# Layer-1 attention with keys and queries projected features-on-partitions, swap and second key form by transfers, rotation on GpSimd, and a new filling of the cells

## The chip, the cores and the metric

The kernel runs on one core of one Trainium2 chip. The metric is device time of one execution in microseconds, the median of several runs. Engines are named as in the profile: PE (TensorE matmul; PEld its weight loads), DVE (VectorE), ACT (ScalarE), POOL (GpSimd), SP (SyncE, which here issues nearly all transfers). Each engine runs its own instructions in order and waits on semaphores.

## The reference

A trunk of two layers over 512 latent tokens and 256 context tokens of width 1024. Layer 0 is a bidirectional mLSTM mixer, layer 1 a windowed attention; each is followed by a squared-ReLU MLP. The change concerns layer 1's mixer only:

```python
def project(u):
    q, k, v = jnp.split(u @ w_in, [1024, 1280], axis=-1)
    # 16 query heads, 4 key/value heads, 64 features each
cq, ck, cv = project(u_ctx)
lq, lk, lv = project(u_lat)
lq = _apply_rope(lq, cos, sin)      # latent tokens only
lk = _apply_rope(lk, cos, sin)

def _apply_rope(x, cos, sin):       # rotate pairs (j, j + 32)
    x1, x2 = x[..., :half], x[..., half:]
    return concatenate([x1 * cs - x2 * sn, x1 * sn + x2 * cs], axis=-1)
```

A block of 128 queries sees the key blocks beside it (distance up to 128) and all 256 context tokens, with a sink logit per head; the result goes through an output projection into the latent stream. Everything is float32; only the latent stream is returned.

## The kernel before

A float32 product is made of three matmuls of rounded halves (`mm3`): high by high, high by low, low by high. A weight unit of 128x1024 comes by a transfer on SP into one of three raw buffers; ACT casts it to whi (L1045) and DVE subtracts wlo (L1046), into one of four split slots. The matmuls of all such products have line L102, that of `mm3`.

Layer 1's mixer begins at the end of layer 0's MLP. `keys_begin` (L1630) projects keys and values of the context, `layer1_mix` (L1643) those of the latent tokens. Tokens lie on the partitions: the tokens' columns are the stationary operand and 256 weight columns move, so a block of 128 tokens gets its keys and values as 128x256 in PSUM (`proj_part`, L1847). In `kv_out` (L1870) and `q_out` (L1896) ACT copies V away; `rope` (L1856) makes two products on DVE and an addition on DVE or POOL (L1867); the result is split in halves (ksp, qsp: ACT cast L1883 and L1901, DVE subtraction L1884 and L1902), which are laid side by side for each head, 64 features of one half and 64 of the other. PE transposes them with identr, 128x128 at a time (48 transposes for the keys in L1890, 64 for the queries in L1907), and the copies ks (L1892) and qs (L1910) fetch them from PSUM. Keys exist in two forms, k0 (high half above, low half below for one, turned round for the other) and k1, so that two matmuls of 128 rows give the three products of halves.

Attention has 16 cells (g, j): head group g of four heads, query block j. `scores` (L1913) makes one head at a time: five or six matmuls into s (L1935 to L1942), the maximum on DVE (L1948), the exponential on ACT into e (L1955), and the division by the sum on POOL (L1966). `weigh` (L1970) transposes e on PE (L1982), copies it to ph on ACT (L1987) and makes the values' matmuls av (L1999, L2005); yb (L2007) and two DVE additions (L2010) put the result together.

The pattern `PAT = "SFTTFSFTFSTFTFSFFVVV"` sets the order within a cell: S a head of scores (five heads ahead of the cell), T transposes of one key block, V values, F a step of filling. The filling of PE's time is other projection work: in cells 0 to 3 the keys and values of head groups 2 and 3 (four steps), in every cell up to 13 the queries of a later cell (four steps of six matmuls of 256 columns, `q_steps`), and from cell 4 on two parts of the output projection of the group before (`out_part`, L1819), six in the last two cells. A scheduler orders each engine's instructions from the order in which the program makes them and from its own estimates of when their inputs are there; each engine then keeps that order.

Of the kernel before, what the change touches and what calls it, by code (L numbers as in the profile page):

```python
# [9 lines left out]
F32 = mybir.dt.float32  # L10
# [42 lines left out]
C_SN = C_CS + 4 * DH  # L53
C_END = C_SN + 4 * DH


class Trunk:
# [1036 lines left out]
    def ffn0(self, hooks, done, pre):  # L1094
# [219 lines left out]
        self.plan += [lambda pr=pr, i=i: self.unit(a["wskv"][pr, i]) for pr in range(2) for i in range(2)]  # L1314
# [315 lines left out]
    def keys_begin(self, u, hooks):  # L1630

        w = self.begun
        self.wkv = [w[:2], w[2:]]
        self.kvc = [self.mm.tile([P, 512], F32, name="pj", tag="mm") for _ in range(2)]
        at = {(1, 4, 0): 0, (1, 4, 2): 1}
        for pr in range(2):
            for j, t in zip((4, 5), self.kvc):
                for i in range(4):
                    self.proj_part(self.wkv[pr], j, self.rows_of(u), 256, i, t[:, 256 * pr:256 * pr + 256])
                    if (pr, j, i) in at:  # L1640
                        hooks[at[pr, j, i]]()

    def layer1_mix(self, u):  # L1643
        nc, tc, a = self.nc, self.tc, self.a
        self.ctx_ada.close()
        with tc.tile_pool(name="sw", bufs=1, reuse_waits="tile") as sw:
            cs = sw.tile([P, 4, DH], F32, name="cs")
            sn = sw.tile([P, 4, DH], F32, name="sn")
            nc.scalar.dma_start(out=cs.rearrange("p b d -> p (b d)"), in_=a["cst"][:, C_CS:C_CS + 4 * DH])
            nc.scalar.dma_start(out=sn.rearrange("p b d -> p (b d)"), in_=a["cst"][:, C_SN:C_SN + 4 * DH])  # L1650
            self.cs, self.sn = cs, sn
# [12 lines left out]
            ks = [sw.tile([P, 2, 2, T], F32R, name=f"ks{pr}") for pr in range(2)]  # L1664
# [5 lines left out]
            self.ptp, self.ptag = self.at, "at"  # L1670
            wkv, kvl = self.wkv, []
            for j, t in zip((4, 5), self.kvc):
                for pr in range(2):
                    kvl.append(self.kv_out(sw, pr, j, t[:, 256 * pr:256 * pr + 256], None))
            pss = [p_.tile([P, 512], F32, name="pj", tag=t_)[:, :256]
                   for p_, t_ in ((self.mm, "mm"), (self.mm, "mm"), (self.at, "at"), (self.at, "at"))]
# [4 lines left out]
            for f in kvl:  # L1681
                f()
            kvl = [self.kv_out(sw, 0, j, pss[j], nc.vector) for j in range(4)]
            late = []
            for j in range(2):
                ps = self.mm.tile([P, 512], F32, name="pj", tag="mm")[:, :256]
                for i in range(4):
                    self.proj_part(wq[0], j, rows, 256, i, ps)
                late.append(self.q_out(sw, 0, j, ps, nc.vector))
                for f in kvl[2 * j:2 * j + 2]:  # L1690
                    f()
            late.pop(0)()
            self.ctx_mm.close()
            with tc.tile_pool(name="sc", bufs=2, space=PSUM, reuse_waits="tile") as sc, \
                    tc.tile_pool(name="pt1", bufs=3, space=PSUM, reuse_waits="tile") as pt, \
                    tc.tile_pool(name="av", bufs=1, space=PSUM, reuse_waits="tile") as av:
                self.ptp, self.ptag = pt, "pt"
                ys = [None] * KVH
                todo = [(g, j) for g in range(KVH) for j in range(4)]
                qtodo = [(g, j) for g in range(KVH) for j in range(4)][2:]  # L1700
                parts = []

                def kv_steps(j):
                    ps = pt.tile([P, 512], F32, name="pj", tag="pt")[:, :256]
                    for i in range(4):
                        self.proj_part(wkv[1], j, rows, 256, i, ps)
                        yield
                    late.append(self.kv_out(sw, 1, j, ps, nc.gpsimd))

                def q_steps():  # L1710

                    if not qtodo:
                        return
# [452 lines left out]
```

## Time and profile before

| | |
|---|---|
| median of 3 runs | 1508.35 us (1508.11 to 1510.21) |
| profiled execution | 1506.92 us |
| its span | 1505.1 us |
| clock of PE, mean | 0.997 of full speed |
| layer-1 mixer in the trace, from its first projection to the last output parts | about 890 to 1172 us |
| first scores | 941.11 us |
| first values' matmuls of cells 0, 1, 13 and 14 | 958.88, 971.90, 1117.85 and 1128.82 us |

Time runs from the start of the span. A row of the profile gives line, engine, operation and the tiles written and read by the program's names; "out<-in". A window's row gives the busy time of each engine in it. A wait's row names what ended it. Since PE holds the sum of the time, one reads what PE does and where it stands.

### The profile page before, as it was taken

Reading aid. Unit: us, or ns where it says so; the run is one execution under the profiler, and the core shown is the slowest. Engines: PE = TensorE matmul, PEld = TensorE weight load, DVE = VectorE, ACT = ScalarE, POOL = GpSimd, SP = SyncE. Lnnn points to the kernel's source line nnn. Section 1 sums busy time; section 2 is a strip of 40 time slices with the busy share of each in tenths; the row PEclk is TensorE's granted clock in tenths of the full one; section 3 lists DMA queues with packets and bytes.
Section 4 is the critical chain, followed back from the end, with each engine's and each line's share of the span. In section 5 each row is a group of like instructions: output and inputs, shape, how many; then the busy total and the mean of one; then the engine's idle time right before and its main releaser. Section 6 shows DMA issues by size and latency. Waiting matters only on the chain.

```text
span 1505.1 us, 23719 instructions
## 1 busy us (share of the span) xinstructions
PE 1489.7 (99%) x9144; PEld 1332.4 (89%) x9145; DVE 1110.2 (74%) x2039; ACT 716.1 (48%) x1445; POOL 269.6 (18%) x275
## 2 busy tenths in 40 slices
PE   9999999999999999999999999999999999999998
PEld 5888898979899999999999999888877988888886
DVE  4986638497897877787777768676777874867697
ACT  4544243443764241432414345665666655545454
POOL 0112021311203223212232220323333000000000
PEclk9999999999999999999999999999999999999999
DMA  9233313245132334343443422010110533240321
GB/s 378 77 98 115 124 58 123 74 144 164 43 99 81 127 115 154 113 154 126 127 154 113 139 71 78 29 48 24 57 43 29 196 112 112 76 148 23 104 71 56
DMA packets 46632, 157.27 MB, mean 104 GB/s; under 512 B 5136, under 2 KB 7696, under 8 KB 46392
## 3 DMA queue, kind: packets, MB, share of 16 engines
q1 hardware_dynamic: 45344, 154.25, 31.1%
q8 instruction: 72, 1.18, 0.3%
q10 hardware_dynamic: 1175, 1.51, 0.3%
q14 instruction: 41, 0.33, 0.1%
HBM read 153.64 MB, written 2.10 MB: 103 GB/s over the span
## 4 chain that ended last, share of the span: by engine, by line
PE 93%; DVE 4%; ACT 2%; issue 1%; POOL 0%; POOLq 0%; DVEq 0%; ACTq 0%
PE mm L102 57%; PE p L102 10%; PE pj L102 5%; PE kept L102 3%; PE pt L1982 2%; PE pb L102 2%; PE pc L102 2%; PE av L1999 2%; PE acc L102 1%; PE at L1001 1%; PE s L1942 1%; PE at L958 1%; PE arow L102 1%; PE at L994 1%; PE s L1937 1%
## 5 line engine op out<-in xcount | busy, mean ns | idle before, releaser
L102 PE MATMUL mm<-h,whi 128*128 128x384 f32 x1024 | 262.5, 337 | 0.0
L1046 DVE TENSOR_TENSOR wlo<-raw,whi 128x1024 fp32r<-128x1024 f32 (+2 forms) x152 | 180.0, 1188 | 78.5 <-ACT whi L1045 76.7
L1045 ACT CAST whi<-raw 128x1024 fp32r<-128x1024 f32 (+2 forms) x152 | 150.9, 998 | 159.0 <-PE mm L102 105.9
L102 PE MATMUL mm<-uH,whi 128*128 128x512 f32 (+1 forms) x496 | 189.3, 386 | 0.0
L102 PE MATMUL mm<-uH,wlo 128*128 128x512 f32 (+1 forms) x496 | 186.7, 377 | 0.0
L102 PE MATMUL mm<-uL,whi 128*128 128x512 f32 (+1 forms) x496 | 186.0, 377 | 0.0
L102 PEld LDWEIGHTS mm<-h,whi 128*128 128x128 f32 x1024 | 185.4, 188 | 0.4 <-DVE h L1046 0.2
L269 DVE SCALAR_TENSOR_TENSOR adap<-raw,crow 128x1024 bf16<-128x1024 f32 x128 | 164.1, 1282 | 13.9 <-DMA raw<-ada 13.0
L102 PE MATMUL mm<-h,wlo 128*128 128x384 f32 x512 | 172.1, 336 | 0.0
L102 PE MATMUL p<-t,whi 128*128 128x384 f32 x448 | 114.2, 336 | 0.0
L1045 ACT CAST whi<-sum 128x512 fp32r<-128x512 f32 (+1 forms) x42 | 31.8, 760 | 162.2 <-PE mm L102 90.7
L102 PEld LDWEIGHTS mm<-uH,wlo 128*128 128x128 f32 x496 | 93.4, 188 | 17.4 <-issue 0.2
L102 PEld LDWEIGHTS mm<-uL,whi 128*128 128x128 f32 x496 | 93.5, 189 | 15.4 <-DVE uL L1091 0.3
L102 PEld LDWEIGHTS mm<-uH,whi 128*128 128x128 f32 x496 | 93.0, 189 | 15.2 <-issue 0.2
L102 PEld LDWEIGHTS mm<-h,wlo 128*128 128x128 f32 x512 | 96.1, 188 | 0.0
L1046 DVE TENSOR_TENSOR wlo<-wb,whi 128x1024 fp32r<-128x1024 f32 x49 | 59.1, 1219 | 36.0 <-ACT whi L1045 35.8
L1046 DVE TENSOR_TENSOR h<-r,h 128x384 fp32r<-128x384 f32 (+2 forms) x100 | 58.7, 589 | 31.2 <-ACT h L1045 30.8
L102 PEld LDWEIGHTS p<-t,whi 128*128 128x128 f32 x448 | 81.2, 188 | 0.0
L1045 ACT CAST whi<-wb 128x1024 fp32r<-128x1024 f32 x49 | 51.6, 1054 | 57.9 <-PE mm L102 48.2
L102 PE MATMUL mm<-uC,whi 128*128 128x256 f32 x416 | 78.2, 287 | 0.3 <-ACT whi L1045 0.3
L1966 POOL TENSOR_SCALAR e<-e,den 128x512 f32<-128x512 f32 (+1 forms) x64 | 51.4, 815 | 139.2 <-DVE den L1964 64.2
L102 PE MATMUL p<-t,wlo 128*128 128x384 f32 x224 | 75.3, 336 | 0.0
(405 smaller groups left out, 3626.2 us busy)
## 6 DMA issues: line engine op xcount, KB each, us to landing
raw<-ada SPq DMA_DIRECT2D x80, 512.0 KB, 3.5
raw<-w SPq DMA_DIRECT2D x64, 512.0 KB, 3.5
raw<-w2a SPq DMA_DIRECT2D x32, 512.0 KB, 3.5
wb<-w2b SPq DMA_DIRECT2D x28, 512.0 KB, 3.5
adaw<-ada SPq DMA_DIRECT2D x16, 512.0 KB, 11.2
raw<-wqk SPq DMA_DIRECT2D x8, 512.0 KB, 4.3
raw<-wv SPq DMA_DIRECT2D x8, 512.0 KB, 4.2
raw<-wo SPq DMA_DIRECT2D x8, 512.0 KB, 3.5
```

The source lines that it names most:

```text
L102: i = self.nc.tensor.matmul(**kw)
L269: self.tc.keep_in_program_order(nc.vector.scalar_tensor_tensor(out=pr, in0=w, scalar=0.5, in1=self.crow[:, v, :], op0=ALU.mult, op1=ALU.mu ...
L958: mm(out=kv[d][64 * h:64 * h + 64, n * VW:(n + 1) * VW], lhsT=kp[:, d, j, 64 * h:64 * h + 64], rhs=v[:, j, h, :], start=True, stop=True)
L994: mm(out=os[d][hh][:, ob], lhsT=qs[d][HP[hh], j * P:(j + 1) * P], rhs=C[HP[hh], n - 1, d, :], start=not started, stop=False)
L1001: mm(out=o[hh][:, i * VW:(i + 1) * VW], lhsT=pw[g, d, hh][:, i, :], rhs=v[:, 3 * g + i, hh, :], start=False, stop=i == 2)
L1045: keep(self.nc.scalar.copy(out=hi, in_=src))
L1046: keep((eng or self.nc.vector).tensor_tensor(out=lo, in0=src, in1=hi.bitcast(F32), op=ALU.subtract))
L1937: mm(out=lat, lhsT=ql, rhs=k0[:, lo * P:hi * P], start=True, stop=False)
L1942: mm(out=lat, lhsT=ql, rhs=k1[:, lo * P:hi * P], start=False, stop=True)
L1966: nc.gpsimd.tensor_scalar(out=out[ii][:, :W], in0=out[ii][:, :W], scalar1=den[:, ii:ii + 1], scalar2=1.0, op0=ALU.mult, op1=ALU.mult)
L1982: nc.tensor.transpose(out=pt[:, i * P:(i + 1) * P], in_=ps_[i][:, n * P:(n + 1) * P], identity=self.ident)
L1999: mm(out=o[i * DH:(i + 1) * DH, :], lhsT=v(n + i), rhs=pq[n + i], start=n == 0, stop=n == len(blks) - 2)
```

## The change

Keys and queries are projected turned: the weight columns (128 features, two heads) are stationary and 512 latent tokens move (256 for the context), so the result lies with features on the partitions (`turned`). V stays as it was (`values`). The weights are laid out for this on the host. No transposes of keys and queries are left; the tables of cosines and sines become 128x512.

Rotation needs each feature beside the one 32 partitions further. In `rope` with late=True (keys and all queries but those of group 0) ACT copies the product from PSUM to rt, four transfers of 32x512 on SP's queue write rx with the halves swapped, and POOL makes the two products and the addition at 128x512. With late=False (the queries of group 0) four ACT copies of 32x512 from PSUM make the swap, and DVE the three operations. `stack` splits two heads: for each an ACT cast of 64x512 and a DVE subtraction of 64x512 into the other 64 partitions. The second key form k1 is the first with its halves exchanged, by two transfers of 64 partitions per pair of heads. Buffers: e 12 to 10, qs now holds a head group (3 buffers), yb has its own two.

The filling is new. Blocks of queries of 128 features (eight steps of three matmuls of 512 columns) stand in cells 0, 1, 2, 3, 4 and 8; the values of blocks 2 and 3 are spread among the first five heads of scores; output parts go to cells 5 to 15 by a table. Matmul columns for K, Q and V are the same in sum: K and Q of the latent tokens are 48 and 192 matmuls of 128x512, V 96 of 128x256.

The order of ACT at the start of the attention, before: ksp and qsp are the split halves, pt the transposes, ks and qs the copies, whi a weight unit's cast, e the exponential of the first scores.

```order
L1045 CAST whi<-raw 128x1024
L1874 COPY vst_9547<-pj 128x128
L1045 CAST whi<-raw 128x1024
L1883 CAST ksp<-rp_9711 128x2x2x64
L1874 COPY vst_9545<-pj 128x128
L1892 COPY ks_9543<-pt 128x4x128
L1892 COPY ks_9542<-pt 128x4x128
L1892 COPY ks_9543<-pt 128x4x128
L1883 CAST ksp<-rp_9720 128x2x2x64
L1892 COPY ks_9542<-pt 128x4x128
L1883 CAST ksp<-rp_9729 128x2x2x64
L1892 COPY ks_9542<-pt 128x4x128
```

The same place after, up to the first exponentials: pk and pq are the products of keys and queries, pj those of the context, rt and rx the rotation's tiles, vst the values.

```order
L1879 CAST ks<-pj 64x256
L1045 CAST whi<-raw 128x1024
L1858 COPY rt<-pk 128x512 x2
L1879 CAST ks<-pj 64x256 x2
L1045 CAST whi<-raw 128x1024 x2
L1879 CAST ks<-rt 64x512 x2
L1864 COPY rx<-pq 32x512 x4
L1879 CAST ks<-rt 64x512 x2
L1864 COPY rx<-pq 32x512 x4
L1879 CAST qs<-rt 64x512 x2
L1673 COPY vst_9543<-pv 128x256
L1673 COPY vst_9544<-pv 128x256
```

The casts of the keys read rt, POOL's result, and stand ahead of the copies rx and the query casts; two whi casts stand ahead of them all.

SP's order at the same place, after (before, the weight units follow each other directly):

```order
L80 DMA raw<-wsq 128x1024 x3
L1887 DMA ks<-ks 64x2x256
L80 DMA raw<-wsq 128x1024
L1887 DMA ks<-ks 64x2x256 x3
L1862 DMA rx<-rt 32x512 x8
L80 DMA raw<-wsq 128x1024 x2
L1887 DMA ks<-ks 64x2x512 x4
L80 DMA raw<-wsq 128x1024 x2
```

The eight swap transfers stand behind the context's second key form, and the latent keys' behind the swaps.

POOL's order from the first rotation on, after. Before, the first thing it does here is the division of e (L1966), with a rotation's addition of 128x128 or 128x256 between groups of them.

```order
L1868 TENSOR_TENSOR rx<-rx,sn 128x512
L1869 TENSOR_TENSOR rt<-rt,cs 128x512
L1870 TENSOR_TENSOR rt<-rt,rx 128x512
L1868 TENSOR_TENSOR rx<-rx,sn 128x512
L1869 TENSOR_TENSOR rt<-rt,cs 128x512
L1870 TENSOR_TENSOR rt<-rt,rx 128x512
L1948 TENSOR_SCALAR e<-e,den 128x512 x4
L1948 TENSOR_SCALAR e<-e,den 128x640 x4
L1868 TENSOR_TENSOR rx<-rx,sn 128x512
L1869 TENSOR_TENSOR rt<-rt,cs 128x512
L1948 TENSOR_SCALAR e<-e,den 128x640 x2
L1870 TENSOR_TENSOR rt<-rt,rx 128x512
```

Six products of 128x512 stand ahead of the first division; later ones stand between the divisions.

The diff, cut to its core:

```diff
 def keys_begin(self, u, hooks):
-        w = self.begun
-        self.wkv = [w[:2], w[2:]]
+        self.wkv = w = self.begun
...
+        xs = self.xs(u)["C"]
+        for b in range(2):
+            self.turned(self.kvc[0][:, 256 * b:256 * b + 256], w[b], xs, 0, KT)
+        for j, at in ((4, slice(0, 256)), (5, slice(256, 512))):
+            for i in range(4):
+                self.values(self.kvc[1][:, at], j, self.rows_of(u), 2 * i, 2 * i + 2)
...
 def layer1_mix(self, u):
...
+            for m in range(2):
+                self.keys_out(m, self.kvc[0][:, m * NCX:(m + 1) * NCX], slice(NL, T))
...
             for kt in range(KT):
-                for j in range(4):
-                    self.proj_part(wkv[0], j, rows, 256, kt, pss[j], 1)
+                for b in range(2):
+                    self.turned(pk[b], self.wkv[b], xl, kt, kt + 1)
             wq = {0: [self.unit(a["wsq"][0, i]) for i in range(2)]}
...
+            rk = [self.rope(sw, pk[m], True) for m in range(2)]
+            for m in range(2):
+                ps = (self.at, self.mm)[m].tile([P, 512], F32, name="pq", tag=("at", "mm")[m])
+                self.turned(ps, wq[0][m], xl, 0, KT)
+                self.keys_out(m, rk[m](), slice(0, NL))
+                self.queries_out(sw, 0, m, self.rope(sw, ps, False))
...
+                qat = {0: (1, 0), 1: (1, 1), 2: (2, 0), 3: (2, 1), 4: (3, 0), 8: (3, 1)}
+                outs = {5: 3, 6: 3, 7: 2, 9: 3, 10: 2, 11: 2, 12: 2, 13: 3, 14: 6, 15: 6}
...
+                    ps = pt.tile([P, 512], F32, name="pq", tag="pt")
+                    for kt in range(KT):
+                        self.turned(ps, wq[g][b], xl, kt, kt + 1)
+                        if kt < KT - 1:
+                            yield
+                    late.append(lambda g=g, b=b, f=self.rope(sw, ps, True): self.queries_out(sw, g, b, f()))
...
                 def filler(n):
-                    fs, late[:] = late[:], []
-                    its = chain(kv_steps(n) if n < 4 else (), q_steps(), out_steps(2 if n < 14 else 6))
...
+                    its = chain(q_steps(*qat[n]) if n in qat else (), out_steps(outs.get(n, 0)))
+                    yield next(its, None)
+                    while late:
+                        late.pop(0)()
                     yield from its
...
-                for _ in range(4):
-                    next(sg)
...
+                fl = chain(v_steps(2, pt, "pt"), v_steps(3, pt, "pt"))
+                for _ in range(5):
+                    next(sg)
+                    next(fl, None)
+                    next(fl, None)
...
+    def turned(self, ps, w, xs, i0, i1):
+        for kt in range(i0, i1):
+            sl = slice(kt * P, (kt + 1) * P)
+            self.mm3(ps, w[0][:, sl], w[1][:, sl], *xs(kt), kt == 0, kt == KT - 1)
...
+    def rope(self, sw, ps, late):
...
+        x, y = [sw.tile([P, NL], F32, name=n, tag=n, bufs=2) for n in ("rt", "rx")]
+        if late:
+            nc.scalar.copy(out=x, in_=ps)
+        for i in range(4):
+            o, r = [slice(32 * k, 32 * k + 32) for k in (i ^ 1, i)]
+            if late:
+                nc.sync.dma_start(out=y[o], in_=x[r])
+            else:
+                nc.scalar.copy(out=y[o], in_=ps[r])
+        def rest():
+            op = (nc.gpsimd if late else nc.vector).tensor_tensor
+            op(out=y, in0=y, in1=self.sn, op=ALU.mult)
+            op(out=x, in0=x if late else ps, in1=self.cs, op=ALU.mult)
+            op(out=x, in0=x, in1=y, op=ALU.add)
+            return x
+        return rest if late else rest()
+
+    def stack(self, outs, x):
+        for e, out in enumerate(outs):
+            r, o = [slice(64 * i, 64 * i + 64) for i in (e, 1 - e)]
+            nc.scalar.copy(out=out[r], in_=x[r])
+            nc.vector.tensor_tensor(out=out[o], in0=x[r], in1=out[r].bitcast(F32), op=ALU.subtract)
+
+    def keys_out(self, m, x, cols):
+        k0, k1 = [self.swd["ks"][:, i, 2 * m:2 * m + 2, cols] for i in range(2)]
+        self.stack([k0[:, e] for e in range(2)], x)
+        for i in range(2):
+            self.nc.sync.dma_start(out=k1[64 - 64 * i:128 - 64 * i].bitcast(F32), in_=k0[64 * i:64 * i + 64].bitcast(F32))
```

The lines of the new functions that the traces name: L1858 the copy rt, L1862 the swap transfers, L1864 the copies rx, L1868 to L1870 the rotation, L1879 and L1880 the halves, L1887 the second key form, L1917 to L1924 the scores, L1930 the maximum, L1937 the exponential, L1948 the division, L1964 the transposes of e, L1969 ph, L1981 and L1987 the values, L1989 yb.

More of the change, by code (lines that the diff above doesn't have):

```diff
@@ L1313, in ffn0 @@
             self.plan += [unit_w2(c, i) for i in range(4)]
-        self.plan += [lambda pr=pr, i=i: self.unit(a["wskv"][pr, i]) for pr in range(2) for i in range(2)]
+        self.plan += [lambda i=i: self.unit(a["wskv"][i]) for i in range(4)]
         self.feed(True)
@@ L1663, in layer1_mix @@
                 msk.append(mk)
[L1664 removed]
+            ks = sw.tile([P, 2, KVH, T], F32R, name="ks")
             vst = [self.base.tile([P, 2, 2, DH], F32, name=f"vst{j}", tag=f"hC{j}") for j in range(NCH)]
@@ L1692, in layer1_mix, with v_steps @@
-            late.pop(0)()
+            rk = [self.rope(sw, pk[m], True) for m in range(2)]
[4 more added lines that the diff above has]
+                self.queries_out(sw, 0, m, self.rope(sw, ps, False))
+            def v_steps(j, pool, tag):
+                ps = pool.tile([P, 512], F32, name="pv", tag=tag)[:, :256]
+                for i in range(0, KT, 2):
+                    self.values(ps, j, rows, i, i + 2)
+                    if i < KT - 2:
+                        yield
+                put(j, ps)
+                yield
@@ L1896, in q_out @@
-    def q_out(self, sw, g, j, ps, eng):
-        nc = self.nc
-        qs = self.swd["qs"]
-        q = self.rope(sw, j, ps, 4, eng)
-        sp = sw.tile([P, 4, 2, DH], F32R, name="qsp", tag="sp", bufs=4)
-        nc.scalar.copy(out=sp[:, :, 0, :], in_=q)
-        nc.vector.tensor_tensor(out=sp[:, :, 1, :], in0=q, in1=sp[:, :, 0, :].bitcast(F32), op=ALU.subtract)
-        def late():
-            pt = self.ptp.tile([P, 512], F32R, name="pt", tag=self.ptag)
-            for i in range(4):
-                nc.tensor.transpose(out=pt[:, i * P:(i + 1) * P],
-                                    in_=sp[:, i].rearrange("p a d -> p (a d)"), identity=self.identr)
-            qs[g, j] = sw.tile([P, 4, P], F32R, name="qs", tag="qs", bufs=5)
-            nc.any.tensor_copy(out=qs[g, j], in_=pt.rearrange("p (h t) -> p h t", t=P))
-        return late
+    def turned(self, ps, w, xs, i0, i1):
+        for kt in range(i0, i1):
+            sl = slice(kt * P, (kt + 1) * P)
+            self.mm3(ps, w[0][:, sl], w[1][:, sl], *xs(kt), kt == 0, kt == KT - 1)
@@ new lines, in values @@
+    def values(self, ps, j, rows, i0, i1):
+        for kt in range(i0, i1):
+            hi, lo = self.wkv[2 + kt // 4]
+            sl = slice(kt % 4 * 256, kt % 4 * 256 + 256)
+            self.mm3(ps, *rows(kt, j), hi[:, sl], lo[:, sl], kt == 0, kt == KT - 1)
+    def rope(self, sw, ps, late):
+        nc = self.nc
+        x, y = [sw.tile([P, NL], F32, name=n, tag=n, bufs=2) for n in ("rt", "rx")]
[14 more added lines that the diff above has]
+        return rest if late else rest()
@@ L1913, in scores, with queries_out @@
+    def queries_out(self, sw, g, m, x):
+        if m == 0:
+            self.swd["qs"][g] = sw.tile([P, 4, NL], F32R, name="qs", tag="qs", bufs=3)
+        q = self.swd["qs"][g]
+        self.stack([q[:, 2 * m + e, :] for e in range(2)], x)
     def scores(self, sw, g, j, scp, out):
@@ L1917, in scores @@
         mm = nc.tensor.matmul
-        q4 = d["qs"][g, j]
-        k0, k1 = [d["ks"][g // 2][:, i, g % 2, :] for i in range(2)]
+        q4 = d["qs"][g][:, :, j * P:(j + 1) * P]
+        k0, k1 = [d["ks"][:, i, g, :] for i in range(2)]
         lo, hi = max(0, j - 1), min(4, j + 2)
```

141 lines of the change are left out of this document (30 added, 111 removed).

## The prediction

> **What bounds the kernel now.** I read the page first, then one table of windows around layer 1's attention, then the timeline of its start, then groups by form. From the page: the busy time of each engine, the granted clock in 40 slices, and the chain that ended last.
>
> ```profile
> PE 1489.7 (99%) x9144; PEld 1332.4 (89%) x9145; DVE 1110.2 (74%) x2039; ACT 716.1 (48%) x1445; POOL 269.6 (18%) x275
> PEclk9999999999999999999999999999999999999999
> PE 93%; DVE 4%; ACT 2%; issue 1%; POOL 0%; POOLq 0%; DVEq 0%; ACTq 0%
> ```
>
> TensorE (PE) is busy 99% at full clock and makes 93% of the chain. So the time is the sum of PE's work, and a change counts by what it takes off PE and by what it makes PE wait. The page's span is 1505.1 us; the profiled execution took 1506.92 us, 1.8 us around the span, and lies 1.4 us under the median of the runs, 1508.35. I work with differences and set them against the median.
>
> The table of windows (us; then each engine's busy time and count, granted clock, DMA share, GB/s). Its rows are the whole stage, the latent half of the first keys projection, a stretch of 512-column matmuls of the last FFN, attention cells 0 to 12, and cell 13:
>
> ```profile
> 890.00:1172.00 282.00, 279.25 (x2018) 236.58 (x2017) 206.98 (x462) 175.29 (x395) 80.08 (x104) 1.00 0.15 48
> 919.10:931.20 12.10, 12.08 (x97) 11.60 (x97) 10.09 (x20) 8.12 (x21) 0.00 (x0) 1.00 0.09 23
> 1232.00:1282.00 50.00, 50.00 (x222) 41.42 (x221) 26.96 (x36) 27.52 (x39) 0.00 (x0) 1.00 0.38 126
> 958.88:1117.85 158.97, 158.33 (x1137) 128.46 (x1136) 110.28 (x257) 102.77 (x235) 48.22 (x64) 1.00 0.14 44
> 1117.85:1128.82 10.97, 10.97 (x71) 8.29 (x71) 8.77 (x21) 7.13 (x16) 4.11 (x4) 1.00 0.15 51
> ```
>
> Even in attention PE stands still for 0.64 us of 159 (158.97 less 158.33), with DVE at 69%, ACT at 65% and POOL at 30%. There is little idle time to win; what can be won is PE work.
>
> **What PE loses.** The timeline of PE before the first scores (start, length, engine, line, how many; in brackets idle time before it and who ended it), and two starts of the keys projection:
>
> ```profile
> 919.05 0.28 PE L102 MATMUL pj<-whi,uH 128*128 128x256 f32 x1
> 919.17 0.28 PE L102 MATMUL pj<-wlo,uH 128*128 128x256 f32 x1
> ...
> 939.29 0.79 PE L1890 MATMUL pt<-identr,ksp 128*128 128x128 f32 x8
> 939.92 0.51 PE L1907 MATMUL pt<-identr,qsp 128*128 128x128 f32 x4
> 941.11 0.38 PE L1935 MATMUL s<-ks,qs 128*128 128x256 f32 x1 [0.68 <-ACT qs L1910]
> ```
>
> (1) Transposes. Eight take 939.92 − 939.29 = 0.63 us, 79 ns each. There are 48 for the keys and 64 for the queries; all 112 go: 112 × 0.079 = **8.8 us**. Nothing hides them, PE has no gaps beside them.
>
> (2) Shape. K and Q move the same number of columns as before, but 480 matmuls of 256 columns become 240 of 512. A 256-column one takes 919.17 − 919.05 = 0.120 us. The nearest row for 512 columns is the FFN's stretch, 50.00/222 = 0.225 us. A pair saves 0.240 − 0.225 = 15 ns, 240 of them **3.6 us**. [...] V (96 matmuls) and the context (96) keep 256 columns.
>
> (3) Small waits. The keys window holds 97 matmuls, 97 × 0.120 = 11.64 us of 12.10: **0.5 us** of waiting for normalised columns (uL), which arrive in time when a column pair is asked for every 6 × 0.225 = 1.36 us. The **0.7 us** before the first scores (the 0.68 above) belongs to the transposed path and goes with it; (4) says what is late there next.
>
> Together 8.8 + 3.6 + 0.5 + 0.7 = **13.6 us** less.
>
> **What the change adds: the first scores.** The rotation's other half now comes by transfers, and its products run on POOL, in order, with ACT in order behind them. Rows for the parts, by form over the whole program, for the stage alone, and from the timeline and the DMA issues:
>
> ```profile
> L1154 POOL TENSOR_TENSOR sum<-raw 128x512 f32<-128x512 f32 x14 | 26.3, 1878 | 53.2 <-DVE t L1046 49.6 <-DVE wlo L1046 3.7
> L1155 POOL TENSOR_TENSOR sum<-raw,sum 128x512 f32<-128x512 f32 x14 | 19.8, 1416 | 1.1
> L1867 POOL TENSOR_TENSOR rp<-rp,rp 128x256 f32<-128x256 f32 x14 | 10.3, 736 | 23.7 <-DVE rp L1866 20.6 <-PE s L1942 3.1
> ```
>
> ```profile
> L302 DVE TENSOR_TENSOR ssL<-ssL,sq 128x512 f32<-128x512 f32 x4 | 2.8, 690 | 0.4 <-ACT sq L298 0.2
> L2007 ACT COPY yb<-av 64x512 f32<-64x512 f32 x16 | 9.3, 583 | 18.2 <-PE av L2005 15.8 <-PE av L1999 2.3
> L1966 POOL TENSOR_SCALAR e<-e,den 128x640 f32<-128x640 f32 x32 | 29.1, 921 | 49.8 <-DVE den L1964 28.9 <-DVE nb L1950 4.7 <-ACT qs L1910 4.6
> ```
>
> ```profile
> 930.03 1.05 ACT L1045 CAST whi<-raw 128x1024 fp32r<-128x1024 f32 x1
> 932.89 1.56 ACT L1892 CAST ks<-pt 128x512 fp32r<-128x512 f32 x3
> ```
>
> ```profile
> 895.69 0.33 SPq L80 DMA_DIRECT2D raw<-wskv  x1
> cs<-cst ACTq DMA_DIRECT2D x1, 128.0 KB, 2.1
> ```
>
> In these rows one POOL product of 128x512 takes 1.42 to 1.88 us, one on DVE 0.69; copies of 512 columns on ACT follow each other every (1.56 − 0.58)/2 = 0.49 us; SP issues a transfer in 0.33 us, and a small one lands after 2.1 us. I work the start in the clock of before:
>
> - PE. The latent keys begin at 919.05 and take 48 × 0.225 = 10.8 us, to 929.9. All four split slots are held by the K and V units until then, so the first q unit's cast (whi, 1.05 us) starts only when PE is through with the first K unit, shortly before the end: PE stands about 0.5 us. Then 48 matmuls of 512 and 52 of 256 columns (Q of head group 0, V of blocks 0 and 1) keep it busy 10.8 + 6.2 = 17.0 us, to **947.4**. Next in its order is the first score.
> - ACT and SP to the swaps. After the second whi at 931.4 come two copies of the K products (to 932.4) and two context casts (to 933.4). On SP, the eight swap transfers stand behind four transfers of the context's second key form and a weight load; the four need DVE's context halves, so the swaps issue from about 934.4, 8 × 0.33 = 2.6 us. The first four land at about 934.4 + 1.3 + 2.1 = 937.8, the rest by 939.2.
> - POOL. Three products per block, in order: at 1.42 us block 0 is done at 942.1, block 1 at **946.3**.
> - ACT again. Its order has two whi casts for head group 1 ahead of the key casts; they wait for Q's last readers (about 942) and end at 943.4. Then two key casts, four copies rx, two key casts that need POOL's block 1, four copies rx, and the query casts. From 946.3: 2 × 0.49 + 4 × 0.49 + 0.49 = 3.4 us, and DVE's lower query half 0.69 us: 950.4. The V copy that frees the scores' PSUM bank stands behind the next casts, up to 1 us more: **950.4 to 951.4**.
>
> PE would wait from 947.4 for 3.0 to 4.0 us. With 1.88 us a product POOL ends 6 × 0.46 = 2.8 us later, and PE waits up to 6.8. If a small swap lands at once (2.1 us less on the first block), up to 2 of the 3 go. I take **4.0**, from the 1.42 row with the later end. Behind it the first transposes of e need max, exp and POOL's 0.92 us in a shorter queue of filler than before: **1.0 us**, between 0 and 2. With the 0.5 above: **5.5 us** at the start.
>
> [...] By DVE's price the six products would take 4.1 instead of 8.5 us and most of this wait would not exist.
>
> **What it adds: inside the loop.** The six later query blocks each cost ACT one copy and two 64-row casts, POOL three products, SP four transfers, DVE two subtractions. In such a cell POOL has four normalisations of 0.92 us or less and 4.3 to 5.6 us of rotation, in some 13 us: it fits. Cells 7 and 10 to 12 get thin, two output parts and no projection; the nearest row is cell 13, quoted above: 10.97 us, PE busy throughout, DVE at 8.77. From a block's last matmul to its query casts I count 0.5 + 1.3 + 2.1 + 4.3 + 1.0 = 9.2 us, and the casts are wanted a cell or more later. The exposed part is ACT: it takes instructions in order, and the casts that wait for POOL stand ahead of exps and of the copies ph. I take **1.3 us** for the loop, between 0 and 3.
>
> **Sum.** −13.6 + 5.5 + 1.3 = **−6.8 us**: profiled about 1500.1, median 1508.35 − 6.8 = **1501.5 us**.
>
> **Rivals.**
> (a) *The start is covered* (swaps land early, ACT's whi casts come early). For: before waits only 0.68 us there. Against: six POOL products in a row with PE holding 17 us of work. Total stalls about 1.5 us: 1508.35 − 13.6 + 1.5 = **1496.3**. Chance 0.20, for stalls under 4 us.
> (b) *The start chain is longer*: products at 1.88, ACT late for the next. Start 5.5 + 2.8 + 2, loop 3: 13.3 us of stalls, **1508**, no change. It needs stalls between 10 and 16 us. Chance 0.18.
> (c) *Slower: POOL's rotation holds ACT in the loop.* One mechanism: in a cell with a query block, a query cast waits on ACT for POOL, the exps behind it wait, POOL's next normalisations wait for the exps, and PE's transposes for those. If each of six blocks holds PE for 3 us: 1508.35 − 13.6 + 5.5 + 18 = **1518**. It turns the sign at (13.6 − 5.5)/6 = 1.4 us a block. For: POOL and ACT are strictly in order, and e has two buffers fewer. Against: scores run five heads, over a cell, ahead, and POOL and ACT are far from full. Chance 0.07.
> (d) *The clock falls after the wait.* If the 4 us wait made PE run at half speed for as long again, PE would do 2 us of work in 4: **1503.5**; chance 0.05. The longest wait in the trace of before is 1.7 us, with PEclk at 9 there:
>
> ```profile
> PE at L901 <- DVE kp L914: 1.7, 1, 1.7
> ```
>
> [...]
>
> **How the numbers follow.** My forecast is stalls of 4 to 10 us, 1499 to 1505, chance 0.50. The range 1496 to 1508 takes in (a)'s centre, (d) and the lower half of (b), and leaves out (c), the upper part of (b) and the best of (a): about 0.18. A measurement tells about 0.2%, 3.0 us, from no change, so faster means under 1505.3 and slower above 1511.4. Faster: 0.50 + 0.20 + 0.05 and 0.05 of (b) = 0.80. Same: 0.13 of (b). Slower: 0.07.
>
> **What would show it.** Right: transposes of 128x128 with identr gone, pq and pk starting every 0.225 us; one wait of PE before the first score, 3 to 5 us, ended by ACT's query cast or DVE's half behind POOL's sixth product; POOL products of 1.4 us; waits of PE in the cells summing to 1 or 2 us. Wrong: no wait before the first score (a), waits in each of the first five cells (c), a granted clock under 1.00 after the first score (d), or 512-column starts at 0.240 us, which takes (2) away.

## The result, and the profile after

The changed kernel takes 1514.96 us (median of 5 runs, 1514.01 to 1516.45), the one before 1508.53 us beside it: ratio 1.0039, 95% interval 1.0025 to 1.0054. It is slower by 6 us where 7 us less were forecast, and lies outside the range. Its profiled execution took 1514.97 us with a span of 1513.1 us, 8.0 us over the span of before.

The page of after, the busy time of the engines and the granted clock in slices of 38 us:

```profile
PE 1485.4 (98%) x8793; PEld 1310.4 (87%) x8793; DVE 1110.8 (73%) x1978; ACT 717.4 (47%) x1428; POOL 289.7 (19%) x281
...
PEclk9999999999999999999999999999999999999999
```

PE has 4.3 us less work than before by this count and the span is 8.0 us longer: PE stands still more. The view of waits says where (who waited for whom: us in total, how often, the longest). For PE:

```profile
PE s L1917 <- ACT vst L1673: 7.5, 1, 7.5
PE s L1917 <- ACT e L1937: 2.8, 3, 1.9
...
PE pt L1964 <- POOL e L1948: 1.3, 1, 1.3
...
PE av L1981 <- ACT ph L1969: 1.1, 1, 1.1
```

and for the engines beside it, from the first latent projection to the end of the attention:

```profile
POOL rx L1868 <- DMA rx<-rt: 49.0, 7, 24.2
...
ACT qs L1879 <- POOL rt L1870: 11.1, 3, 5.6
```

The one wait of PE before the first scores was forecast at 4.0 us and is 7.5; it ends with ACT's copy vst, the last link of the chain that the prediction drew. ACT stands 11.1 us in the loop for POOL's rotation. The start, in the timeline of SP, POOL, DVE and ACT (a row of several instructions runs from the first to the end of the last):

```profile
932.43 4.11 SPq L1887 DMA_DIRECT2D ks<-ks  x3
936.64 5.02 SPq L1862 DMA_DIRECT2D rx<-rt  x8
```

```profile
940.68 1.28 POOL L1868 TENSOR_TENSOR rx<-rx,sn 128x512 f32<-128x512 f32 x1 [24.22 <-DMA rx<-rt]
941.93 1.29 POOL L1869 TENSOR_TENSOR rt<-rt,cs 128x512 f32<-128x512 f32 x1
943.29 1.30 POOL L1870 TENSOR_TENSOR rt<-rt,rx 128x512 f32<-128x512 f32 x1
944.55 2.28 POOL L1868 TENSOR_TENSOR rx<-rx,sn 128x512 f32<-128x512 f32 x1
946.79 1.73 POOL L1869 TENSOR_TENSOR rt<-rt,cs 128x512 f32<-128x512 f32 x1
948.59 1.60 POOL L1870 TENSOR_TENSOR rt<-rt,rx 128x512 f32<-128x512 f32 x1
```

```profile
945.71 3.36 DVE L1880 TENSOR_TENSOR ks<-rt,ks 64x512 fp32r<-64x512 f32 x2
949.10 1.64 DVE L1868 TENSOR_TENSOR rx<-rx,sn 128x512 f32<-128x512 f32 x1
950.77 0.69 DVE L1869 TENSOR_TENSOR rt<-pq,cs 128x512 f32<-128x512 f32 x1
951.50 0.68 DVE L1880 TENSOR_TENSOR ks<-rt,ks 64x512 fp32r<-64x512 f32 x1
```

```profile
942.54 1.05 ACT L1045 CAST whi<-raw 128x1024 fp32r<-128x1024 f32 x1 [4.39 <-PE pq L102]
944.63 1.26 ACT L1879 CAST ks<-rt 64x512 fp32r<-64x512 f32 x2 [1.04 <-POOL rt L1870]
945.92 2.35 ACT L1864 COPY rx<-pq 32x512 f32<-32x512 f32 x4
950.23 1.26 ACT L1879 CAST ks<-rt 64x512 fp32r<-64x512 f32 x2 [1.96 <-POOL rt L1870]
951.51 2.34 ACT L1864 COPY rx<-pq 32x512 f32<-32x512 f32 x4
953.87 1.26 ACT L1879 CAST qs<-rt 64x512 fp32r<-64x512 f32 x2
955.15 0.65 ACT L1673 COPY vst<-pv 128x256 f32<-128x256 f32 x2
```

The chain is the forecast one, link by link, and each link is longer: the swaps issue every 0.63 us, not 0.33; POOL starts at 940.7; its second block takes 5.6 us and not 4.3, and while it runs DVE's subtraction takes 1.68 us where it takes 0.68 once POOL is done (951.50); ACT's short copies follow each other every 0.59 to 0.63 us, not 0.49. The first score starts at 955.58. The granted clock, which the page's slices hide, in windows of the wait, behind it, and at the second place where it falls:

```profile
948.00:955.50 7.50, 0.07 (x1) 0.00 (x0) 7.02 (x9) 5.38 (x11) 2.11 (x2) 0.81 0.54 122
955.60:959.40 3.80, 3.80 (x18) 3.61 (x18) 3.02 (x5) 1.43 (x3) 0.00 (x0) 0.50 0.48 166
959.40:966.00 6.60, 6.60 (x55) 6.40 (x55) 4.21 (x8) 3.72 (x9) 1.37 (x2) 1.00 0.01 2
1031.10:1034.50 3.40, 1.52 (x10) 1.24 (x10) 2.81 (x5) 2.32 (x5) 2.54 (x3) 1.00 0.00 0
1034.50:1037.90 3.40, 3.40 (x9) 1.34 (x9) 1.63 (x6) 2.86 (x8) 1.55 (x2) 0.50 0.03 10
```

### The profile page after: what moved, and what is told of

The parts are those of the page before. It is cut to its first block, busy times and chain, and to the rows that moved or that the text cites. A ratio compares the mean times of both kernels' runs of the same rounds, so it can differ in the third digit from the quotient of the medians.

```text
span 1513.1 us, 23024 instructions
## 1 busy us (share of the span) xinstructions
PE 1485.4 (98%) x8793; PEld 1310.4 (87%) x8793; DVE 1110.8 (73%) x1978; ACT 717.4 (47%) x1428; POOL 289.7 (19%) x281
## 4 chain that ended last, share of the span: by engine, by line
PE 89%; DVE 4%; ACT 2%; POOL 2%; issue 1%; DMA 1%; SPq 0%; POOLq 0%; ACTq 0%; DVEq 0%
PE mm L102 56%; PE p L102 10%; PE kept L102 3%; PE pb L102 2%; PE pc L102 2%; PE av L1981 2%; PE pt L1964 2%; PE pq L102 1%; PE acc L102 1%; PE at L1001 1%; PE s L1924 1%; PE arow L102 1%; PE at L958 1%; PE pk L102 1%; PE wps L102 1%
## 5 line engine op out<-in xcount | busy, mean ns | idle before, releaser
L1046 DVE TENSOR_TENSOR wlo<-raw,whi 128x1024 fp32r<-128x1024 f32 (+2 forms) x152 | 183.8, 1213 | 97.9 <-ACT whi L1045 94.4
L1948 POOL TENSOR_SCALAR e<-e,den 128x512 f32<-128x512 f32 (+1 forms) x64 | 49.9, 792 | 101.6 <-DVE den L1946 50.5
```

The source lines that it names most:

```text
L1046: keep((eng or self.nc.vector).tensor_tensor(out=lo, in0=src, in1=hi.bitcast(F32), op=ALU.subtract))
L1948: nc.gpsimd.tensor_scalar(out=out[ii][:, :W], in0=out[ii][:, :W], scalar1=den[:, ii:ii + 1], scalar2=1.0, op0=ALU.mult, op1=ALU.mult)
```

## The experiments

The theory after the result: the saving on PE is there; it is lost before the first score (transfers, POOL, ACT in one chain), in the loop (POOL's rotation, for which ACT waits), and to the clock. The rival: the new shapes and filling themselves cost the time, and waits only show it. To set the runs side by side I measure three stretches of PE's timeline in each trace: from the first latent key matmul (pk) to the first score, from there to the first values' matmul (av), and from there to the first matmul of the next normalisation (at, L315). In after these four starts are 919.38, 955.58, 976.83 and 1164.53 us.

| run | K swap, products | loop's swap, products | pins | pk to s | s to av | av to at | median us | ratio |
|---|---|---|---|---|---|---|---|---|
| after | transfers, POOL | transfers, POOL | no | 36.20 | 21.25 | 187.70 | 1514.96 | 1.0039 |
| e4_dve | transfers, DVE | transfers, DVE | no | 34.31 | 18.41 | 181.09 | 1505.14 | 0.9971 |
| e10_local_pool | ACT, POOL | ACT, POOL | no | 31.33 | 21.19 | 185.18 | 1508.53 | 0.9998 |
| e6_both | ACT, DVE | ACT, DVE | no | 29.87 | 20.29 | 183.35 | 1503.92 | 0.9969 |
| e1_k_local | ACT, DVE | transfers, POOL | no | 29.87 | 20.27 | 186.56 | 1507.01 | 0.9992 |
| e2_q_local | transfers, POOL | ACT, DVE | no | 36.08 | 21.11 | 182.44 | 1511.37 | 1.0019 |
| e9_k_local_dve | ACT, DVE | transfers, DVE | no | 29.87 | 20.29 | 177.46 | 1499.36 | 0.9937 |
| e11_pinned | ACT, DVE | transfers, DVE | yes | 29.87 | 20.30 | 176.66 | 1498.58 | 0.9932 |
| e12_pool_pinned | ACT, DVE | transfers, POOL | yes | 29.87 | 20.29 | 184.12 | 1504.14 | 0.9974 |

The stretches come from one profiled execution each, the ratios from all runs against the kernel before. In one row the first two stretches hold other work than in the rest: in e4_dve PE's order has all 96 matmuls of V ahead of the first score (48 to 52 elsewhere) and 38 matmuls of scores ahead of the first values (50 elsewhere). Only the sum of its first two stretches can be set beside the others, and that sum is about 12 × 0.13 = 1.6 us too good, by an estimate from the 302 matmuls of scores in the loop, which follow each other every 0.13 us.

**Keys local.** The keys take the path that the queries of group 0 have already.

```diff
-            rk = [self.rope(sw, pk[m], True) for m in range(2)]
+            rk = [lambda r=self.rope(sw, pk[m], False): r for m in range(2)]
```

> The keys alone are rotated without transfers and POOL (four ACT copies of 32x512 out of PSUM make the swap, DVE the three products); the queries of the loop stay as changed. Theory (the K rotation's chain on SP, POOL and ACT makes PE wait 7.5 us before the first score, and the granted clock is halved for some us behind it): the wait falls to under 1.5 us and the clock stays at 1.00 at 956 to 959 us, so 7.5 + 2 less: about 1506, ratio to before 0.998 to 0.999. Rival (the new filling and shapes cost the time, the wait only moves it): the wait reappears at the first transposes of e, about 1513 to 1515.

Measured 1507.01 us, ratio 0.9992 (0.9983 to 1.0001). The wait before the first score fell to 1.6 us (under 1.5 was expected) and the matmuls of 256 columns behind it follow each other every 0.12 us, where the changed kernel at half clock has 0.21, as the theory had it; the waits in the loop stayed. Start and ramp are 6.3 + 1.0 us shorter. The rival falls for this part: the wait did not come back elsewhere.

**Loop's queries local.**

```diff
-  late.append(lambda g=g, b=b, f=self.rope(sw, ps, True): self.queries_out(sw, g, b, f()))
+  late.append(lambda g=g, b=b, f=self.rope(sw, ps, False): self.queries_out(sw, g, b, f))
```

> Only the six query blocks of the loop are rotated without transfers and POOL; the keys stay as changed. Theory (ACT stands for POOL's rotation ahead of exps and copies ph, 11 us of ACT waits): waits of PE in the cells fall from about 6 us to under 2 and the second stretch of half clock (1034 to 1038 us) goes: about 1509 to 1510; the 7.5 us before the first score stay. Rival (four more ACT copies of 0.58 us and three DVE products per block load ACT and DVE just as much): 1514 to 1516.

Measured 1511.37 us, ratio 1.0019 (1.0010 to 1.0029). The loop is 5.3 us shorter in the trace and the mean clock of that execution is 0.996 against 0.994 in after; 7.4 us of waiting before the first score stay. The median lies above the 1509 to 1510 that the theory gave, and further from the rival's 1514 to 1516.

**Both local.** The two edits together.

> Keys and all queries are rotated without transfers and POOL. Theory: both gains add: 1515 - 9.5 - 5 = about 1500, ratio 0.993 to 0.996. Rival (ACT becomes the bound in cells with a query block, with 4.6 us of copies and casts more in a block): 1506 or more.

Measured 1503.92 us, ratio 0.9969 (0.9956 to 0.9982). Against the changed kernel that is 11.0 us, nearly the 8.0 and 3.6 of the two runs added: the gains add, and each is smaller than the theory had it, which gave 1500. In the loop ACT's extra copies have a price, which the mixed run below shows (183.35 us with them, 177.46 without).

**The clock, first try.** Values of block 1 made again, into the other half of their PSUM tile.

```diff
                 self.values(ps[:, :256], j, rows, 0, KT)
                 put(j, ps[:, :256])
+                for n in (KT, KT, 3)[3 - 3 * j:]:
+                    for kt in range(n):
...
+                        self.mm3(ps[:, 256:], *rows(kt, j), hi[:, sl], lo[:, sl], kt == 0, kt == n - 1)
```

> As the changed kernel, but PE multiplies 57 matmuls of 256 columns more (values of block 1 again, into the unused half of their PSUM bank) in the 7.5 us in which it waits: 6.8 us of extra work that nobody reads. Theory (the idle time itself halves the clock): the first score comes at the same time, the granted clock is 1.00 from 956 to 959 us, and the total is 1.5 to 2 us under the changed kernel: about 1513. Rival (the clock falls for another reason, or the half clock costs nothing because others are late): 1515, the same as the changed kernel.

Measured 1523.26 us, ratio 1.0093 (1.0077 to 1.0109), where 1513 was expected. It says nothing on the clock: the extra matmuls waited themselves for the copy of block 1's values (7.9 us) and ran behind the wait, partly at half clock (starts every 0.21 us up to 958.4, every 0.12 us from 958.6 on).

**The clock, second try.** The repetitions stand ahead of the copy.

```diff
+                for n in (3, KT, KT, KT)[3 - 3 * j:]:
+                    for kt in range(n):
...
+                        self.mm3(ps, *rows(kt, j), hi[:, sl], lo[:, sl], kt == 0, kt == n - 1)
                 put(j, ps)
```

> The test of the clock once more, since the extra matmuls of the run before waited themselves for the copy of block 1's values and ran behind the wait. Now 57 matmuls of 256 columns (6.8 us, block 1's values made three times, nobody reads the first two) stand ahead of that copy, where PE would wait. Theory (idle time halves the clock): first score within 0.5 us of 955.6, granted clock 1.00 at 956 to 959 us, total 1.5 to 2 us under the changed kernel: about 1513, ratio 1.0027. Rival (the half clock costs nothing): 1515.

Windows of that run, where PE would have waited and at the first scores:

```profile
950.00:957.00 7.00, 6.98 (x59) 6.78 (x57) 6.54 (x8) 4.85 (x9) 2.30 (x2) 1.00 0.50 112
957.80:961.60 3.80, 3.80 (x32) 3.70 (x33) 3.01 (x5) 1.61 (x3) 0.00 (x0) 1.00 0.53 170
```

With PE busy the clock stays at 1.00, 32 matmuls instead of 18 in the 3.8 us behind the first score. So it was the idle time that halved the clock there. But the run took 1516.48 us, ratio 1.0050 (1.0035 to 1.0065), no faster than the changed kernel, and from the first score to the first values went 20.58 us instead of 21.25: 0.7 us, or 1.2 when one allows for the four more matmuls of V of 0.12 us that stand in this stretch here. My expectation of 1.5 to 2 us falls. That maximum, exponential and division bind there, so that most of what the slow PE loses was waiting anyway, is a guess that no run tests.

**Products on DVE.** One word of the code.

```diff
-            op = (nc.gpsimd if late else nc.vector).tensor_tensor
+            op = nc.vector.tensor_tensor
```

> Swaps by transfers as in the changed kernel, but all products of the rotation on DVE instead of POOL (one word of the code). Theory (POOL's products, slowed further where DVE runs beside them, are most of the chain before the first score and of ACT's waits in the loop): six products of 0.69 us end about 4 to 5 us earlier, PE waits 2 to 4 us before the first score, no product or subtraction takes over 1.3 us, and the loop's waits shrink to 1 to 3 us: 1505 to 1508, ratio 0.998 to 1.000. Rival (the transfers on SP's queue, landing at 940.7 us, are the chain): PE still waits 6 us or more, 1512 to 1514.

Measured 1505.14 us, ratio 0.9971 (0.9960 to 0.9982): from 6 us slower to 3 us faster, with every transfer in place. Up to the first values it gains 4.7 us (57.45 to 52.72), in the loop 6.6; with the 1.6 us of scores that stand in the loop here, about 3.1 and 8.2. The one word changed more than the engine: the scheduler also moved 44 matmuls of V ahead of the first score, and the wait expected there came as 2.4 us ahead of the third head. The run "best of both" makes the same exchange with PE's order all but unchanged.

**Values first.** Blocks 2 and 3 of V ahead of the first score.

```diff
-                for _ in range(5):
-                    next(sg)
-                    next(fl, None)
-                    next(fl, None)
+                for _ in fl:
+                    pass
+                for _ in range(5):
+                    next(sg)
```

> As the changed kernel, but the values of blocks 2 and 3 (88 more matmuls of 256 columns, 10.6 us) stand on PE ahead of the first score instead of between the first five heads. Theory (PE merely runs out of work before the keys and queries are there): no wait and full clock before the first score, which comes at about 958.5 us, and 1 to 4 us of new waits for maximum and exponentials behind it, since nothing fills there: 1506 to 1510. Rival (the time is lost by the engines beside PE, and only shows elsewhere): waits of 7 us or more behind the first scores, 1514 or more.

Measured 1514.05 us, ratio 1.0034 (1.0020 to 1.0048), as the changed kernel, where 1506 to 1510 was expected. The edit moves 44 matmuls of V, 5.3 us, and not the 88 and 10.6 us of the expectation. PE got 2.3 us further and then waited 5.2 us with block 2's values, since their PSUM bank too is freed by the copies vst on ACT. The cover that I had in mind doesn't exist; as a test of the ramp the run is inconclusive.

**Casts later.** The query casts pinned on ACT behind what the program makes before them, two or four filling steps later.

```diff
-                    yield next(its, None)
-                    while late:
-                        late.pop(0)()
+                    fs, late[:] = late[:], []
+                    for _ in range(3 if n == 2 else 5):
+                        yield next(its, None)
+                    for f in fs:
+                        f()
...
-            nc.scalar.copy(out=out[r], in_=x[r])
+            (self.tc.keep_in_program_order if pin else lambda i: i)(nc.scalar.copy(out=out[r], in_=x[r]))
```

> As the changed kernel (swaps by transfers, POOL's rotation), but in the loop the query casts are pinned on ACT behind the exponentials and copies ph that the program makes before them, two or four filling steps later. Theory (ACT in order is what passes POOL's lateness on to PE): ACT's waits for POOL fall from 11 us to under 4, PE's waits in the cells from about 6 to under 3 and the second stretch of half clock goes: 1510 to 1512. Rival (POOL's contention with DVE and its late divisions of e hold PE): 1514 to 1516.

Measured 1513.77 us, ratio 1.0035 (1.0022 to 1.0047). In its trace the loop is 182.8 us, 4.9 less, and the mean clock was 0.993 against 0.994 in after; in the runs nothing is left that can be told from the changed kernel (1510 to 1512 was expected). In the trace 1.4 us are lost again in the first two stretches (36.50 and 22.35 us) and 2.7 outside the three, where layer 0 has two stretches of half clock (last section). ACT's waits for POOL fell to 6.9 us, not under 4. So the order on ACT is a part of it at most.

**The fourth corner.** Swaps by ACT copies, products on POOL.

```diff
-            if late:
-                nc.sync.dma_start(out=y[o], in_=x[r])
-            else:
-                nc.scalar.copy(out=y[o], in_=ps[r])
+            nc.scalar.copy(out=y[o], in_=ps[r])
```

> The fourth corner of transfers or ACT copies against POOL or DVE: swaps by ACT copies out of PSUM (one copy rt and four rx a block), products on POOL. Theory (POOL's products and the waiting for them in order are the larger part): PE still waits 2.5 to 5 us before the first score, ACT still waits for POOL in the loop, 1509 to 1513, ratio 1.001 to 1.003. Rival (the transfers through SP are the larger part): 1504 to 1506, near the run with both local.

Measured 1508.53 us, ratio 0.9998 (0.9989 to 1.0007), between the two expectations. With it the table can be read both ways. Up to the first values (the first two stretches together) the transfers cost 4.9 us with products on POOL (57.45 less 52.52) and 2.6 with products on DVE (52.72 less 50.16); POOL costs 4.7 with transfers and 2.4 with ACT copies (52.52 less 50.16). In the loop POOL costs 6.6 with transfers and 1.8 with ACT copies. With the 1.6 us of scores put back, the three numbers that use e4_dve become about 4.2, 3.1 and 8.2.

**Best of both.** Keys local, all products on DVE, the loop's swaps by transfers; then with the pins of the run "casts later" on top.

```diff
-            rk = [self.rope(sw, pk[m], True) for m in range(2)]
+            rk = [lambda r=self.rope(sw, pk[m], False): r for m in range(2)]
...
-            op = (nc.gpsimd if late else nc.vector).tensor_tensor
+            op = nc.vector.tensor_tensor
```

> The two useful undoings together: keys rotated out of PSUM without transfers, all products on DVE, and the swaps of the loop's queries still by transfers. Theory (what is lost lies in two places, the chain before the first score and POOL's rotation in the loop): first score as early as in the run with keys and queries both local, the loop as short as in the run with all products on DVE: about 1501 to 1503, ratio 0.995 to 0.997, the fastest of all. Rival (the remaining time is bound elsewhere, in ACT's order): 1504 to 1505, no better than either.

> The first of this call, and the loop's query casts pinned on ACT behind the exponentials and copies made before them. Theory (ACT in order passes lateness on): 0 to 1.5 us less than without the pins, 1500 to 1502. Rival (with the products on DVE nothing waits long any more): the same within 0.5 us.

Measured 1499.36 us, ratio 0.9937 (0.9923 to 0.9950), and 1498.58 us, 0.9932 (0.9919 to 0.9944). Both beat both kernels; the pins are worth 0.8 us, within the noise of the runs. In the loop, with the products on DVE, transfers are better than ACT copies: 177.46 against 183.35 us. Against "keys local" the first differs in the engine of the loop's products alone: 7.7 us of the medians, 9.1 of the loop's stretch. The rival of the first paragraph, that the new shapes and filling cost the time, falls with it: both runs keep the new shapes, the new filling and the ten buffers e. What PE still waits for up to the end of the loop in the second, and ACT for the rotation:

```profile
PE s L1919 <- ACT vst L1673: 1.6, 1, 1.6
...
PE pq L102 <- ACT whi L1045: 0.2, 1, 0.2
```

```profile
ACT qs L1881 <- DVE rt L1872: 3.0, 4, 1.4
```

**POOL or the order.** The pinned one with the loop's products on POOL again.

```diff
-            op = nc.vector.tensor_tensor
+            op = (nc.gpsimd if late else nc.vector).tensor_tensor
```

> Keys local and casts pinned as in the fastest run, but the loop's rotation on POOL again: it differs from that run in the engine of the loop's products alone, and from the run with only the keys local in the pins alone. What it tells apart is how much of the loop's loss is ACT's waiting in order and how much POOL itself. If both: the stretch from the first values to the next normalisation takes 181 to 183 us (186.6 without pins, 176.7 with DVE) and the total is 1502 to 1504. If the order on ACT is all: 177 to 178 us and 1499. If POOL itself is all: 185 to 187 us and 1506 to 1507.

Measured 1504.14 us, ratio 0.9974 (0.9965 to 0.9983), the loop 184.12 us, both just above what was expected if the order and POOL count together: the pins give 2.4 us (186.56 less 184.12), and POOL by itself 7.5 (184.12 less 176.66). The split is rough. The loop of this trace has a stretch at half clock, which can cost up to 1.7 us:

```profile
1022.30:1025.70 3.40, 3.40 (x12) 2.32 (x10) 2.76 (x7) 2.27 (x6) 0.96 (x2) 0.50 0.00 0
```

The run "casts later" has the same edits in the loop and takes 182.82 us there; by it the pins give 3.7 and POOL 6.2. ACT still waits 6.9 us for POOL there:

```profile
ACT qs L1881 <- POOL rt L1872: 6.9, 3, 3.3
```

What of POOL's 6 to 7.5 us is this wait and what the contention shown below was not separated.

## Why the prediction was wrong

**What PE loses: right.** The transposes are gone and the shapes cost what the rows said. The fastest run has the same PE instructions as the changed kernel and almost no waits; from the first projection of the mixer (at 905.71 us before; the 890 in the table of before lies ahead of it) to the next normalisation it takes 240.16 us, against 250.89 before and 258.50 after. That is 10.7 us less with 1.8 us of waits left, so 12.5 of the 13.6 us. The 48 matmuls of 512 columns of the keys follow each other in (930.06 − 919.38)/47 = 0.227 us for the forecast 0.225:

```profile
919.38 0.40 PE L102 MATMUL pk<-uH,whi 128*128 128x512 f32 x1
919.61 0.40 PE L102 MATMUL pk<-uL,whi 128*128 128x512 f32 x1
...
930.06 0.39 PE L102 MATMUL pk<-uH,wlo 128*128 128x512 f32 x1
```

**What it adds: both terms too small.** Between the changed kernel and the fastest run lie 18.3 us: 6.3 before the first score, 1.0 to the first values, 11.0 in the loop. The forecast had 5.5 for the first two and 1.3 for the third. With the 1.8 us of waits that the fastest run keeps, the first two cost 9.1 us. With the start as measured and the loop as forecast the change would still have been faster, by 12.5 − 9.1 − 1.3 = 2.1 us; it is the loop that turns the sign.

*The loop, 11.0 us for 1.3, is the step that failed.* "It fits", the prediction said, from POOL's busy time in a cell, and took ACT's exposure at 1.3 us. Busy time was the wrong question: POOL works 70 of the loop's 188 us, it was not full, but late and in the way. Here is the longest case. ACT has a query cast next and waits 5.64 us; the copy ph that PE's values need stands behind it, and PE waits 1.1 us for that and 0.8 for the exponential behind it:

```profile
1012.05 0.59 ACT L1969 COPY ph<-pt 128x512 f32<-128x512 f32 x1 [0.23 <-PE pt L1964]
1018.27 1.26 ACT L1879 CAST qs<-rt 64x512 fp32r<-64x512 f32 x2 [5.64 <-POOL rt L1870]
1019.55 0.59 ACT L1969 COPY ph<-pt 128x512 f32<-128x512 f32 x1
```

```profile
1020.19 1.07 PE L1981 MATMUL av<-ph,vst 128*64 128x512 f32 x2 [1.10 <-ACT ph L1969]
...
1022.05 0.39 PE L1917 MATMUL s<-ks,qs 128*128 128x256 f32 x1 [0.79 <-ACT e L1937]
```

```profile
1013.14 1.28 POOL L1868 TENSOR_TENSOR rx<-rx,sn 128x512 f32<-128x512 f32 x1 [4.43 <-DMA rx<-rt]
1014.38 1.28 POOL L1869 TENSOR_TENSOR rt<-rt,cs 128x512 f32<-128x512 f32 x1
1015.64 1.36 POOL L1948 TENSOR_SCALAR e<-e,den 128x512 f32<-128x512 f32 x2
1016.97 1.26 POOL L1870 TENSOR_TENSOR rt<-rt,rx 128x512 f32<-128x512 f32 x1
```

POOL itself stands 4.43 us for the transfers before its first product, and a division stands between its second and third.

The loss is not spread over the six blocks. From the first values' matmul of one cell to that of the next, in us:

| cell | 0 | 1 | 2 | 3 | 4 |
|---|---|---|---|---|---|
| after | 12.85 | 12.80 | 14.68 | 18.99 | 12.73 |
| e11_pinned | 12.73 | 12.65 | 12.35 | 12.45 | 11.35 |

Cells 2 to 4 hold 10.2 of the 11.0 us, cell 3 alone 6.5. Why the blocks in the other cells cost next to nothing was not tried. Of the 11.0 us PE's rows of waits name 5.9 (2.8, 1.3, 1.1 and 0.7, the last for the output parts mm), and the half clock at 1034.5 can hold up to 1.7; the rest is not named by the view of waits.

This is rival (c), priced at 18 us with a chance of 0.07 and turning the sign at 1.4 us a block. It came in kind, at 1.8 us a block in the mean (11.0/6), but not in each block, as it supposed, nor in each of the first five cells, which was its sign. The argument against it, that scores run five heads ahead, holds for the queries themselves: PE never waited for a query in the loop. It does not hold for the exponentials and copies that stand behind the query cast on ACT, which belong to the next few us.

*The start, 7.5 us of waiting for 4.0.* The mechanism was right and the sizes were off: the swaps were late by 2.6 us (POOL starts at 940.7, where 937.8 was forecast in the clock of before, whose keys begin 0.3 us earlier), since eight issues took 5.02 us and not 2.6 and the context's three before them 4.11; POOL's second block took 5.6 us and not 4.3 beside DVE; short ACT copies cost 0.6 us and not 0.49. Why the issues stand 0.6 us apart on SP was not tried. By the table, 4.2 to 4.9 us of the time up to the first values belong to the transfers and 2.4 to 3.1 to POOL. Two small sums of the prediction are off in the last digit (six starts of 0.225 us make 1.35, the last swaps land at 939.1); nothing hangs on them.

**Rivals.** (a) did not come. (b), the longer chain, came at the start, and (c) in the loop. (d) came too: after the 7.5 us wait the clock was 0.50 for 3.8 us of work and then back at 1.00. Elsewhere it took no such wait: from 1031.1 PE was busy 1.52 of 3.40 us and in the next 3.40 us the clock was 0.50, and in the run with local swaps and products on POOL it fell behind a wait of 2.7 us:

```profile
951.10:954.50 3.40, 3.40 (x18) 3.31 (x17) 2.65 (x5) 1.24 (x2) 0.00 (x0) 0.50 0.43 154
```

At the start the half clock cost 0.7 to 1.2 us and not 2.

**The rows against the change.** The rows of before, 1.42 to 1.88 us for a product on POOL and 0.69 on DVE, were set side by side and then outweighed by POOL's free time. The exchange of the two engines, one word of the code, tried twice, settles it for this kernel: 10 us with the keys by transfers (1514.96 against 1505.14, PE's order changed with it) and 7.7 with the keys local and PE's order all but unchanged (1507.01 against 1499.36).

## What to carry to other kernels

An engine with free time is not a free engine: ask who waits in order behind its result, and put the wait of that instruction, not the busy time, into the sum. Where a chain of transfers, a slow engine and a strictly ordered one ends at the bound engine, price each link with the nearest row of the same shape and neighbourhood; here three links were 20 to 90% longer than rows taken from quieter places. Transfers cost where the next step stands on them (the first keys, 4.2 to 4.9 us); in the loop they paid with the products on DVE (177.46 against 183.35 us) and not with the products on POOL (187.70 against 185.18).

## What the runs showed of the hardware

POOL and DVE held each other up where both worked at the start of the attention. DVE's subtraction of 64x512 took 1.68 us beside POOL's products and 0.69 without (3.36 for two, and 0.68, above); POOL's product 2.28 beside DVE and 1.28 alone. Some of DVE's smallest operations ended only with an instruction of POOL. The addition es, of two elements, in before, after, and the fastest run, e11_pinned (least, median and greatest ns):

```profile
L1960 DVE TENSOR_TENSOR es<-nb,sm x32: 149/161/741, 944.1 to 1138.3; 128x2 f32<-128x2 f32 x32
```

```profile
L1942 DVE TENSOR_TENSOR es<-nb,sm x32: 147/161/1237, 961.2 to 1146.2; 128x2 f32<-128x2 f32 x32
```

```profile
L1944 DVE TENSOR_TENSOR es<-nb,sm x32: 143/160/163, 954.4 to 1128.0; 128x2 f32<-128x2 f32 x32
```

In before and after five of the 64 take over 0.5 us, the others 0.16 or less; each of the five began while POOL was at work and ended within 0.02 us of the end of POOL's instruction. The greatest of before, 0.74 us, ends at 1011.89 beside two divisions (1010.31 to 1011.88), that of after, 1.24 us, at 1029.12 beside a product of 128x512 (1027.39 to 1029.10). In the fastest run POOL makes divisions alone, and es takes 0.16 us at most; the subtractions qs take up to 1.17 us there, with a median of 0.69. The trace of before held this already in its greatest values (0.74 us); the mean hides it. Why the two engines hold each other up, no run shows.

The half clock also comes without any change near it: in the trace of the run with the casts later, two stretches of 3.4 us in layer 0 have it, where before and after show 1.00:

```profile
309.50:312.90 3.40, 3.40 (x31) 3.06 (x32) 1.88 (x5) 0.54 (x2) 0.00 (x0) 0.50 0.22 79
405.00:408.40 3.40, 3.40 (x19) 3.40 (x18) 1.00 (x1) 0.00 (x0) 1.88 (x1) 0.50 0.77 216
```

So the clock differed between these executions where the code is the same. Outside the three stretches of the table the variants of the changed kernel run the same code, and their profiled executions take between 1267.1 us (e12_pool_pinned) and 1270.8 us (e1_k_local) there: the total of a single profile is good to about 4 us, not better.
